# Scaling the attention probabilities on one engine, and copying two levels of linear-attention scores on another

## The chip, the cores and the metric

The kernel runs as one launch on one core of one Trainium2 chip. The metric is the device time of that launch in microseconds (us). Engine names are those of the profile: PE is TensorE (matrix products), DVE is VectorE, ACT is ScalarE, POOL is GpSimd, SP issues DMAs.

## The reference, cut to what matters

The reference is a two-layer decoder trunk on 512 tokens of 1024 features. In each layer three mixers share one input projection and one output projection, and a SwiGLU feed-forward network follows. Two of the mixers matter here.

- **Attention.** Eight heads of 64 columns, in two key groups. Each head has a compressed branch and two full causal branches ("selected" and "window"; with these sizes both see all earlier tokens). For a full branch the output is `gate * softmax(q k^T + causal mask) v`.
- **Gated linear attention (GLA).** Four heads of 32 key and 64 value columns. Inside a block of tokens the score of query i against key j is `sum_d q[i,d] k[j,d] exp(b[i,d] - b[j,d])` for j <= i, with b the running sum of the log-decays; the score matrix then multiplies v.

```
s = jnp.einsum('bqghd,bkgd->bghqk', qb, kwb)
p = masked_softmax(s, wmask[None, None, None])
o_win = jnp.einsum('bghqk,bkgd->bqghd', p.astype(vwb.dtype), vwb)
...
return gb[..., 0:1] * o_cmp + gb[..., 1:2] * o_slc + gb[..., 2:3] * o_win
...
decay = jnp.exp(jnp.where(causal[None, None, :, :, None], diff, -jnp.inf))
attn = jnp.einsum('bhik,bhjk,bhijk->bhij', qc, kc, decay)
o_intra = jnp.einsum('bhij,bhjv->bhiv', attn, vc)
```

## The kernel before, in words

All of the work lies in one function, `trunk_kernel`; `mixer(l, ...)` holds a layer's mixers, `out_proj` the output projection and `ffn` the feed-forward network. Weights come in as float32 tiles, and each is split into a high and a low part, the high one by ACT (L270) and the low one by DVE (L273), so that three products on PE (L285 to L287) give one accurate product. Instruction order is not written by hand: the framework takes program order as priority, moves the weight splits and the evacuations of projections ahead by a fixed offset, and fills each engine's queue by a list schedule. Each engine then works through its queue in order. So matmuls of a projection (L285 to L287) stand between the matmuls of GLA and of attention, as filler.

**GLA.** Each layer has four tiles of 128 tokens (loop over t at L681). DVE forms, for each of seven "levels" (64, 32, 16, 8, 4, 2, 1), a scaled query `xq` (L704) and, for four levels at a time, the scaled keys (L705). For each level one product `xk[level] x xq[level]` (L713) puts 128 keys x (4 heads x 64 queries) of scores into a PSUM bank with tag "t" (two banks in turn). DVE then copies the scores into the matrix `at` under a uint8 mask (L716, `copy_predicated`). The diagonal goes into `at` ahead of that, also on DVE (L708). `at` has two buffers, used in turn; each was set to zero once. Then `at` multiplies the values on PE (L723). At level 64 the masked region is one rectangle: keys 0 to 63 against queries 64 to 127. At level 32 it is two: keys 0 to 31 against queries 32 to 63, and keys 64 to 95 against queries 96 to 127. From level 16 on it is four or more.

ACT's part in a tile: three exponentials (L688), four copies that build the block-diagonal query `qbd` (L691), and the copies L725 and L730.

**Attention.** For each of 8 heads and 2 branches, four query tiles i = 0 to 3 of 128 x 128(i+1) keys: scores on PE (L913, L931 to L933), row maximum on DVE (L917, L935), exponential with row sum on ACT (L921, L937) into a probability tile `P`. DVE then forms the factor `rr`, gate over row sum (L942, L943), and the four tiles are scaled by their column of `rr`:

```
for i in SORD:                       # SORD = (0, 1, 2, 3)
    if i in ISP:                     # ISP = (3,)
        nc.gpsimd.tensor_tensor(ps_[i], ps_[i], rr[:, i : i + 1].to_broadcast(...), op=ALU.mult)   # L946
    else:
        nc.vector.tensor_scalar(ps_[i], ps_[i], rr[:, i : i + 1], None, op0=ALU.mult)              # L948
```

PE transposes the scaled tiles (L954), ACT and DVE split them (L255, L256), PE multiplies with the values (L967, L968). The transposes of key block 0 come first, and they read all four tiles.

Of the kernel before, what the change touches and what calls it, by code (L numbers as in the profile page):

```python
# [16 lines left out]
ALU = mybir.AluOpType  # L17
AX = mybir.AxisListType

P = 128  # L20
# [11 lines left out]
GH = 4  # L32
# [19 lines left out]
NBOTH = 2  # L52
ISP = (3,)
PBK = {"g": 2, "s": 3, "t": 2, "o": 1}
# [7 lines left out]
def shape_constants():  # L62
    """Tables that depend on shapes alone: identity, masks, rotary angles, decay selectors."""
    half = HD // 2
# [15 lines left out]
    i = np.arange(P)  # L80
    tsel = np.zeros((P, 9, P), np.float32)
    lmask = np.zeros((P, 7, 64), np.float32)
    for l, s in enumerate(LEVELS):
        for t in range(P):
            b = t // (2 * s) * (2 * s)
            m = b + s
# [36 lines left out]
def trunk_kernel(ctx: ExitStack, tc: tile.TileContext, a, out):  # L123
# [21 lines left out]

# [1 line left out]
    ident = cp.tile([P, P], F32, name="ident")  # L147
# [77 lines left out]

# [1 line left out]

    def rsqrt(dst, v, n):
        """dst = 1/sqrt(v), v > 0, on [P, n] float32."""
        half_v = small(max(n, NT), "nv", 2)[:, 0:n]  # L230
        nc.vector.tensor_scalar(half_v, v, -0.5, None, op0=ALU.mult)
        ib = small(max(n, NT), "ni", 2, I32)[:, 0:n]
        nc.vector.tensor_scalar(ib, v.bitcast(I32), 1, None, op0=ALU.logical_shift_right)
        nc.vector.tensor_scalar(ib, ib, -1, 0x5F3759DF, op0=ALU.mult, op1=ALU.add)
        y = ib.bitcast(F32)
        t = small(max(n, NT), "nt", 2)[:, 0:n]
        for it in range(3):
            if n == 1:
                nc.vector.scalar_tensor_tensor(t, y, half_v, y, op0=ALU.mult, op1=ALU.mult)
            else:  # L240
                nc.vector.tensor_tensor(t, y, y, op=ALU.mult)
                nc.vector.tensor_tensor(t, t, half_v, op=ALU.mult)
            d = dst if it == 2 else y
            nc.vector.scalar_tensor_tensor(d, t, 1.5, y, op0=ALU.add, op1=ALU.mult)
# [31 lines left out]
    def w_rows(mat, r0, nk, c0, w, pri=WPRI, raw=None, hl=None):  # L276
        """rows r0.. as nk K-tiles of w columns."""
        def loads(raw):
            nc.sync.dma_start(raw[:, 0 : nk * w].rearrange("p (k c) -> p k c", k=nk),
                              mat[r0 : r0 + nk * P, c0 : c0 + w].rearrange("(k p) c -> p k c", p=P))  # L280
        hl = w_unit(nk * w, loads, pri, raw, hl)
        return hl[:, :, 0 : nk * w].rearrange("p s (k c) -> p s k c", k=nk)
# [6 lines left out]
    class Norm:  # L289
        """Sum of squares over features, gathered tile by tile; then 1/rms in both layouts."""  # L290

# [30 lines left out]

# [1 line left out]
    class TokNorm(Norm):  # L324
        """The first norm: sums of squares from x as it comes, token-major."""

# [53 lines left out]
    def residual_out(m, ps, gcols, kts, nrm):  # L380
        """xT[m] += ps, and the next norm's operands from it."""
        nc.vector.tensor_tensor(xT[:, m, :], xT[:, m, :], ps, op=ALU.add)  # L382
        if nrm is not None:
            nrm.add(xT[:, m, :])
            if kts is not None:
                split_scaled(kts[m // 2], m % 2, xT[:, m, :], gcols[:, m : m + 1])

    def o_transposed(src, kt):
        """token-major [P, t, 256] -> kt, feature-major hi/lo."""
        for kk in range(2):  # L390
            ps = psum("t")
            for t in range(NT):
                nc.tensor.transpose(ps[:, t * P : (t + 1) * P], src[:, t, kk * P : (kk + 1) * P], ident)
            split_psum(kt[:, kk, 0, :], kt[:, kk, 1, :], ps)

# [1 line left out]
    def mixer(l, norm, xkt, eu=None):  # L397
# [14 lines left out]
        def proj_tok(units, width, evac, tags="gggg", before=None):  # L412
            """units: list of (view [P, 2, nk, w], first K-tile)."""
            ks = [(u, k0, kk) for u, k0, nk in units for kk in range(nk)]
# [11 lines left out]
        def proj_feat(c0, evac):  # L426
            """two neighbouring 128-column tiles, feature-major."""
            us = [w_rows(w_in, k0 * P, 4, c0, 256) for k0 in (0, 4)]
# [16 lines left out]
        with tc.tile_pool(name=f"mx{l}", bufs=1, reuse_waits="tile") as mp:  # L445
# [13 lines left out]
            with tc.tile_pool(name=f"ma{l}", bufs=1, reuse_waits="tile") as ap:  # L459
                # spatial gating  # L460
                uv = ap.tile([P, NT, SEQ], F32, name=nm("uv"))
# [23 lines left out]
                rb = norm.broadcast()  # L485
                # compressed-branch projections, feature-major
                kvT = [ap.tile([P, SEQ], F32, name=nm("kvT")) for _ in range(2)]
# [30 lines left out]

                # compressed keys and values
                hts = []  # L520
# [71 lines left out]
            with tc.tile_pool(name=f"mg{l}", bufs=1, reuse_waits="tile") as gp:  # L592
# [31 lines left out]

                # decay logits and their log-sigmoid
                zps = psum("s")
# [54 lines left out]
                for t in range(NT):  # L681
# [7 lines left out]
                    for h in range(GH):  # L689
                        r = slice(32 * h, 32 * h + 32)  # L690
                        nc.scalar.copy(qbd[r, h, :], qkT[0][r, tk])  # L691
                    # query side of a level first: the key side then takes its factors' place
                    xqs = []
# [16 lines left out]
                    for lv, s in enumerate(LEVELS):  # L710
                        nb = 64 // s
                        ps = psum("t")[:, 0:256]
                        nc.tensor.matmul(ps, xk[:, lv, :], xqs[lv].rearrange("p h i -> p (h i)"), start=True, stop=True)  # L713
                        av = at.rearrange("p h (b u s) -> p h b u s", u=2, s=s)[:, :, :, 1, :]
                        mv = lmask[:, lv, :].rearrange("p (b s) -> p b s", s=s).unsqueeze(1).to_broadcast([P, GH, nb, s])
                        nc.vector.copy_predicated(av, mv, ps.rearrange("p (h b s) -> p h b s", h=GH, s=s))  # L716
# [34 lines left out]

            # selected and window branches: keys and values
            def ev_b(t, ps):
# [25 lines left out]

# [1 line left out]
            with tc.tile_pool(name=f"mt{l}", bufs=1, reuse_waits="tile") as tp_:  # L781
# [108 lines left out]
                for hp in range(H // 2):  # L890
# [4 lines left out]
                    for hh in range(2):  # L895
# [5 lines left out]
                        for br in range(2):  # L901
# [42 lines left out]
                            for i in SORD:  # L944
                                if i in ISP:
                                    nc.gpsimd.tensor_tensor(ps_[i], ps_[i], rr[:, i : i + 1].to_broadcast([P, P * (i + 1)]), op=ALU.mult)  # L946
                                else:
                                    nc.vector.tensor_scalar(ps_[i], ps_[i], rr[:, i : i + 1], None, op0=ALU.mult)  # L948
                            for js in JG:
# [35 lines left out]
    def out_proj(l, okt, k0, kts, nrm, tags=None):  # L985
        tags = tags or ATAGS
        """xT += rows k0 .. k0 + 3 of the output projection."""
        site("o%d" % k0)
# [18 lines left out]
    def down_tok(l, xt, f0, acts):  # L1007
        """Token-major: xt += one part of the down projection."""
        for h in range(2):
# [12 lines left out]
    def finish(l, fp, xt, f0, acts):  # L1022
        """Token-major: the last part of the down projection, and the final norm."""
        nk = len(acts)
# [117 lines left out]
```

## Time and profile before

| what | value |
|---|---|
| median of 3 runs | 1379.78 us (1379.19 to 1382.06) |
| span of the profiled execution | 1392.3 us |
| PE busy | 1349.9 us, 97% of the span |
| DVE busy | 865.5 us, 62% |
| ACT busy | 533.4 us, 38% |
| POOL busy | 192.9 us, 14% |

The profile is of one execution, and its own time is its span of 1392.3 us; the runs give no separate time for that execution. It is 12.5 us (0.9%) over the median of the three timed runs. Layer 0 has its GLA tiles at about 125 to 167 us and its attention at about 205 to 310 us; layer 1 has them at about 811 to 853 us and 891 to 996 us. The feed-forward networks lie at about 340 to 720 us and from 1031 us on. A busy PE is not a PE at its peak: matmuls are pipelined and their ends are modelled.

### The profile page before, as it was taken

What the parts mean: (1) busy time and instruction counts of PE and PEld (TensorE: products, weight loads), DVE (VectorE), ACT (ScalarE), POOL (GpSimd) and SP (SyncE); (2) the same over time, 40 slices, a digit from 0 to 9 for tenths busy, and PEclk for the clock granted to TensorE, in tenths of its full rate; (3) what the DMA queues carried; (4) which work ended last, traced back from release to release, by engine and by line L of the source; (5) the groups of instructions that cost most, each with busy time, mean ns of one, the idle gap of its engine ahead of it and who ended that gap; (6) DMA issues with size and microseconds to landing.
All of it is one profiled execution on the core that took longest, in us unless ns stands there. A gap on an engine that the chain in (4) does not pass through costs nothing.

```text
span 1392.3 us, 17128 instructions
## 1 busy us (share of the span) xinstructions
PE 1349.9 (97%) x6499; PEld 1098.5 (79%) x6499; DVE 865.5 (62%) x1479; ACT 533.4 (38%) x1020; POOL 192.9 (14%) x166
## 2 busy tenths in 40 slices
PE   7999999999999999999999999999999999999997
PEld 6888776777887888788788777767778888888886
DVE  5546889986554455345654478899765535543455
ACT  6234336664332223123441432567553213222232
POOL 2111021113110011001211111111131100110112
PEclk9889999999999999999997999999999999999999
DMA  8422031002333333332362312200133224323321
GB/s 293 111 80 61 16 107 31 16 16 76 91 105 92 91 106 92 91 93 86 100 186 76 91 33 61 77 16 17 36 89 103 91 76 121 92 90 102 96 90 61
DMA packets 160069, 116.84 MB, mean 84 GB/s; under 512 B 7786, under 2 KB 146804, under 8 KB 159988
## 3 DMA queue, kind: packets, MB, share of 16 engines
q1 hardware_dynamic: 155536, 111.53, 26.9%
q10 hardware_dynamic: 4452, 4.23, 1.0%
q8 instruction: 51, 0.84, 0.2%
q14 instruction: 30, 0.25, 0.1%
HBM read 113.65 MB, written 2.10 MB: 83 GB/s over the span
## 4 chain that ended last, share of the span: by engine, by line
PE 80%; DVE 12%; ACT 4%; issue 3%; DMA 1%; POOL 0%; ACTq 0%; SPq 0%; DVEq 0%
PE psg L285 10%; PE psg L286 10%; PE psg L287 10%; PE pss L285 7%; PE pss L286 7%; PE pss L287 7%; PE pst L286 4%; PE pst L285 4%; PE pst L287 4%; PE pso L543 3%; DVE hl L273 2%; PE pst L954 2%; PE pst L713 2%; ACT hl L270 1%; PE pso L967 1%
## 5 line engine op out<-in xcount | busy, mean ns | idle before, releaser
L270 ACT CAST hl<-raw 128x1024 fp32r<-128x1024 f32 (+2 forms) x186 | 192.8, 1036 | 407.3 <-issue 146.4
L273 DVE TENSOR_TENSOR hl<-raw,hl 128x1024 fp32r<-128x1024 f32 (+2 forms) x186 | 269.0, 1447 | 112.6 <-ACT hl L270 111.5
L285 PE MATMUL psg<-kt,hl 128*128 128x512 f32 x520 | 208.1, 401 | 3.4 <-DVE xT L382 3.4
L286 PE MATMUL psg<-kt,hl 128*128 128x512 f32 x520 | 207.8, 400 | 0.0
L287 PE MATMUL psg<-kt,hl 128*128 128x512 f32 x520 | 207.0, 398 | 0.0
L286 PE MATMUL pss<-kt,hl 128*128 128x512 f32 x376 | 146.7, 390 | 0.0
L285 PE MATMUL pss<-kt,hl 128*128 128x512 f32 x376 | 146.4, 389 | 0.0
L287 PE MATMUL pss<-kt,hl 128*128 128x512 f32 x376 | 146.3, 389 | 0.0
L1087 POOL TENSOR_TENSOR ft<-ft,ft 128x512 f32<-128x512 f32 x44 | 56.7, 1288 | 600.9 <-DVE ft L1086 588.2
L285 PEld LDWEIGHTS psg<-kt,hl 128*128 128x128 f32 x520 | 99.0, 191 | 22.9 <-DVE xT L382 4.2
L286 PEld LDWEIGHTS psg<-kt,hl 128*128 128x128 f32 x520 | 99.4, 191 | 19.4 <-issue 0.5
L287 PEld LDWEIGHTS psg<-kt,hl 128*128 128x128 f32 x520 | 99.3, 191 | 19.1
L1086 DVE SCALAR_TENSOR_TENSOR ft<-pss,rb 128x512 f32<-128x512 f32 x44 | 30.4, 691 | 128.0 <-PE pss L287 128.0
L285 PE MATMUL psg<-hl,kt 128*128 128x512 f32 (+2 forms) x288 | 107.2, 374 | 1.3 <-ACT hl L270 0.8
L286 PE MATMUL psg<-hl,kt 128*128 128x512 f32 (+2 forms) x288 | 105.1, 366 | 0.0
L287 PE MATMUL psg<-hl,kt 128*128 128x512 f32 (+2 forms) x288 | 105.1, 366 | 0.0
L285 PEld LDWEIGHTS pss<-kt,hl 128*128 128x128 f32 x376 | 70.6, 188 | 14.6
L287 PEld LDWEIGHTS pss<-kt,hl 128*128 128x128 f32 x376 | 70.6, 188 | 14.4
L286 PEld LDWEIGHTS pss<-kt,hl 128*128 128x128 f32 x376 | 70.6, 188 | 14.4
L255 ACT CAST act<-ft 128x512 fp32r<-128x512 f32 x44 | 27.4, 622 | 115.2 <-DVE ft L1088 115.2
L285 PE MATMUL pst<-act,hl 128*128 128x512 f32 x176 | 69.5, 396 | 0.8 <-ACT act L255 0.8
L286 PE MATMUL pst<-act,hl 128*128 128x512 f32 x176 | 69.9, 397 | 0.3
(330 smaller groups left out, 2502.0 us busy)
## 6 DMA issues: line engine op xcount, KB each, us to landing
raw<-in_w_gate_dram SPq DMA_DIRECT2D x44, 512.0 KB, 3.9
raw<-in_w_up_dram SPq DMA_DIRECT2D x44, 512.0 KB, 3.9
raw<-in_w_down_dram SPq DMA_DIRECT2D x38, 512.0 KB, 3.8
raw<-in_w_in_dram SPq DMA_DIRECT2D x32, 512.0 KB, 3.7
raw<-in_w_out_dram SPq DMA_DIRECT2D x16, 512.0 KB, 3.9
w<-in_cmp_w_k_dram SPq DMA_DIRECT2D x16, 256.0 KB, 4.5
w<-in_cmp_w_v_dram SPq DMA_DIRECT2D x16, 256.0 KB, 2.7
raw<-in_w_down_dram SPq DMA_DIRECT2D x8, 384.0 KB, 3.3
```

The source lines that it names most:

```text
L255: nc.scalar.copy(hi, src)
L270: nc.scalar.copy(hl[:, 0, 0:n], raw[:, 0:n])
L273: e_.tensor_tensor(hl[:, 1, 0:n], raw[:, 0:n], hl[:, 0, 0:n].bitcast(F32), op=ALU.subtract)
L285: nc.tensor.matmul(ps, lh, rh, start=start, stop=False)
L286: nc.tensor.matmul(ps, lh, rl, start=False, stop=False)
L287: nc.tensor.matmul(ps, ll, rh, start=False, stop=stop)
L543: nc.tensor.matmul(ps[:, hh * 62 : (hh + 1) * 62], wu[:, kk, hh * P : (hh + 1) * P], bf[:, s, :], start=s == 0 and hh == 0, stop=s == 15 a ...
L713: nc.tensor.matmul(ps, xk[:, lv, :], xqs[lv].rearrange("p h i -> p (h i)"), start=True, stop=True)
L954: nc.tensor.transpose(T[:, c : c + P], ps_[i][:, j * P : (j + 1) * P], ident)
L967: nc.tensor.matmul(O[:, j * P : SEQ], lhs, pt[:, 0, c : c + n], start=first, stop=False)
L1086: nc.vector.scalar_tensor_tensor(ux, pss[1], 0.5, rb, op0=ALU.mult, op1=ALU.mult)
L1087: nc.gpsimd.tensor_tensor(ux, ux, gx, op=ALU.mult)
```

## The change

Two edits. First, all four probability tiles of a branch are scaled by DVE with the same `tensor_scalar`; the POOL instruction is gone (32 in all: 8 heads x 2 branches x 2 layers). Second, at levels 64 and 32 the scores are copied from PSUM into `at` by ACT, one plain copy for each rectangle (one of 64 partitions x 256 elements, two of 32 partitions x 128 elements), in place of a masked copy of 128 x 256 by DVE (16 masked copies become 24 plain ones: 2 layers x 4 tiles). The rest of the difference is comments and docstrings, left out here; they only shift the line numbers.

```diff
-ISP = (3,)
...
                         av = at.rearrange("p h (b u s) -> p h b u s", u=2, s=s)[:, :, :, 1, :]
+                        if lv < 2:
+                            for b_ in range(nb):
+                                kr_ = slice(2 * s * b_, 2 * s * b_ + s)
+                                nc.scalar.copy(av[kr_, :, b_, :], ps[kr_].rearrange("p (h b s) -> p h b s", h=GH, s=s)[:, :, b_, :])
+                            continue
                         mv = lmask[:, lv, :].rearrange("p (b s) -> p b s", s=s).unsqueeze(1).to_broadcast([P, GH, nb, s])
                         nc.vector.copy_predicated(av, mv, ps.rearrange("p (h b s) -> p h b s", h=GH, s=s))
...
                             for i in SORD:
-                                if i in ISP:
-                                    nc.gpsimd.tensor_tensor(ps_[i], ps_[i], rr[:, i : i + 1].to_broadcast([P, P * (i + 1)]), op=ALU.mult)
-                                else:
-                                    nc.vector.tensor_scalar(ps_[i], ps_[i], rr[:, i : i + 1], None, op0=ALU.mult)
+                                nc.vector.tensor_scalar(ps_[i], ps_[i], rr[:, i : i + 1], None, op0=ALU.mult)
```

## Rows read from the trace of the kernel before

**Rows 1.** The page: span, busy slices, and the chain that ended last.
```profile
span 1392.3 us, 17128 instructions
...
PE   7999999999999999999999999999999999999997
...
PE 80%; DVE 12%; ACT 4%; issue 3%; DMA 1%; POOL 0%; ACTq 0%; SPq 0%; DVEq 0%
```
**Rows 2.** Windows by stage: length, then each engine's busy us, PE clock, DMA.
```profile
125.00:167.00 42.00, 41.10 (x189) 30.51 (x188) 36.59 (x93) 11.40 (x34) 1.59 (x2) 1.00 0.06 19
811.00:853.00 42.00, 41.09 (x189) 30.53 (x189) 36.72 (x93) 11.25 (x33) 1.59 (x2) 1.00 0.06 21
...
205.00:310.00 105.00, 100.52 (x584) 76.13 (x583) 98.10 (x223) 71.67 (x202) 17.71 (x16) 1.00 0.08 25
340.00:720.00 380.00, 378.86 (x1662) 309.71 (x1661) 190.75 (x218) 110.20 (x140) 40.49 (x30) 1.00 0.35 101
891.00:996.00 105.00, 100.61 (x586) 76.35 (x586) 98.44 (x223) 72.08 (x202) 17.72 (x16) 1.00 0.08 25
```
**Rows 3.** The chain by line, in 125 to 167 us and in 205 to 310 us.
```profile
by line: PE pst L713 26.0%; DVE at L716 11.4%; PE psg L285 10.6%; PE psg L286 9.5%; PE psg L287 8.8%; PE pso L723 7.3%; DVE xq L704 4.1%; PE pso L721 3.6%; DVE E L705 3.0%; DVE hl L273 2.9%; PE pst L732 2.6%; issue 1.6%; DVE at L708 1.6%; P
...
by line: PE pst L954 11.8%; PE pso L967 8.3%; DVE P L948 7.5%; PE pso L968 7.0%; DVE PT L256 5.4%; PE psg L285 5.1%; PE psg L287 4.9%; PE psg L286 4.7%; ACT PT L255 4.3%; PE pss L931 4.0%; PE pss L932 3.9%; issue 3.6%; DVE qst L831 3.2%; PE
```
**Rows 4.** The masked copies on DVE: their group, then two lines of DVE's timeline.
```profile
L716 DVE COPY_PREDICATED at<-m,pst 128x256 f32<-128x256 uint8 x56 | 28.8, 514 | 1.7 <-PE pst L713 1.0
...
129.28 0.44 DVE L716 COPY_PREDICATED at<-m,pst 128x256 f32<-128x256 uint8 x1
129.61 0.41 DVE L704 TENSOR_TENSOR xq<-qbd,E 128x256 f32<-128x256 f32 x1
```
**Rows 5.** Copies from PSUM on ACT, by line and shape: busy us, mean ns, idle before.
```profile
L725 ACT COPY osb<-pso 128x256 f32<-128x256 f32 x8 | 3.0, 372 | 9.2 <-PE pso L723 9.2
...
L730 ACT COPY tmp<-pst 128x128 f32<-128x128 f32 x6 | 1.6, 266 | 12.6 <-PE pst L728 12.6
```
**Rows 6.** Waits of DVE for ACT in 205 to 310 us: total us, times, longest.
```profile
DVE PT L256 <- ACT PT L255: 3.6, 9, 1.0
```
**Rows 7.** The scalings: DVE's and POOL's groups, then L948 with min/median/max ns.
```profile
L948 DVE TENSOR_SCALAR P<-P,rr 128x128 f32<-128x128 f32 x32 | 15.1, 472 | 0.4
L948 DVE TENSOR_SCALAR P<-P,rr 128x256 f32<-128x256 f32 x32 | 14.5, 454 | 0.0
L948 DVE TENSOR_SCALAR P<-P,rr 128x384 f32<-128x384 f32 x32 | 13.1, 409 | 0.0
...
L946 POOL TENSOR_TENSOR P<-P,rr 128x512 f32<-128x512 f32 x32 | 35.4, 1107 | 174.5 <-DVE rr L943 134.5 <-ACT P L937 22.5 <-ACT hl L270 10.1
...
L948 DVE TENSOR_SCALAR P<-P,rr x96: 274/405/1131, 210.4 to 994.2; 128x128 f32<-128x128 f32 x32, 128x256 f32<-128x256 f32 x32, 128x384 f32<-128x384 f32 x32
```
**Rows 8.** Timeline of DVE: three scalings (128, 256, 384 columns), POOL idle beside them.
```profile
275.34 0.87 DVE L948 TENSOR_SCALAR P<-P,rr 128x128 f32<-128x128 f32 x3
276.13 1.14 DVE L935 TENSOR_REDUCE nmx<-pss 128x1 f32<-128x384 f32 x2
```
**Rows 9.** Timelines of DVE and of POOL: the same three scalings, POOL busy beside them.
```profile
304.07 1.66 DVE L948 TENSOR_SCALAR P<-P,rr 128x128 f32<-128x128 f32 x3
305.65 0.16 DVE L942 RECIPROCAL rr<-den 128x4 f32<-128x4 f32 x1
...
304.20 1.05 POOL L946 TENSOR_TENSOR P<-P,rr 128x512 f32<-128x512 f32 x1 [8.22 <-DVE rr L943]
```
**Rows 10.** DVE's group of the same operation at 512 columns.
```profile
L1056 DVE TENSOR_SCALAR xt<-yg,rstd 128x512 f32<-128x512 f32 x4 | 1.9, 487 | 0.4
```
**Rows 11.** Waits of PE for the scalings in 205 to 310 us.
```profile
PEld pst L954 <- DVE P L948: 2.0, 4, 0.8
...
PE pst L954 <- DVE P L948: 1.3, 3, 0.6
```
**Rows 12.** Timeline of ACT in a GLA tile: four copies of L691 in a row.
```profile
131.03 1.26 ACT L691 COPY qbd<-gqk 32x128 f32<-32x128 f32 x4 [4.78 <-DVE xq L704]
```

## The prediction, made before the changed kernel was run

> **What bounds the kernel now.** I read the page first [rows 1]: PE is at least nine tenths busy in nearly every slice, and the chain that ended last is 80% PE and 12% DVE, with POOL at 0%. Next come the windows by stage [rows 2]. The reader is to see that the change falls into stages of their own. In a feed-forward stretch PE is busy 378.9 of 380 us and DVE only half of it, so nothing that DVE saves there could be felt, and the change touches nothing there. In each GLA stage (42 us) PE is busy 41.1 us and DVE 36.6; in each attention stage (105 us) PE 100.5 and DVE 98.1. Both engines are close to full, and which of them ends last must be read from the chain within the stage [rows 3]. In GLA the PE lines that the row names sum to 68.4% of the 42 us, the masked copies L716 hold 11.4%, and the other DVE lines named 11.6%. In attention PE leads again, and the scalings L948 hold 7.5% of 105 us.
>
> From this I take a rule for pricing DVE's work: the share of a line's busy time that lies on the chain. L716 is busy 28.8 us in all [rows 4], 14.4 in a layer, and 11.4% of 42 us is 4.8 us on the chain: 33%. L948 is busy 15.1 + 14.5 + 13.1 = 42.7 us [rows 7], 21.4 in a layer, and 7.5% of 105 us is 7.9 us: 37%. The rest of either has PE's in-order stream of filler products beside it.
>
> The sum is made in differences against the profiled execution, whose own time is its span of 1392.3 us [rows 1]; that is 12.5 us above the median of the runs, 1379.78 us. I apply the difference to the median. A measurement of this kernel can tell about 0.2% from no change: 2.8 us.
>
> **GLA: 16 masked copies leave DVE.** Of the seven copies of a tile, those of levels 64 and 32 go. A masked copy runs 0.44 us, and the next DVE instruction starts 0.33 us after it [rows 4]: DVE is freed 16 x 0.33 = 5.3 us. On the chain 33% of that counts: -1.8 us. The ends: nothing (PE's filler alone sets the pace) and the whole -5.3.
>
> ACT gains 24 copies. The trace has no such copy of 64 or 32 partitions; the nearest are copies from PSUM of 256 columns, 372 ns, and of 128 columns, 266 ns [rows 5]. A tile costs ACT 0.37 + 2 x 0.27 = 0.91 us, 3.6 in a layer. ACT is busy 11.4 of 42 us there [rows 2], so I cost this time at nothing: idle ACT hides it. Where that cover is gone, it is 7.2 us over both layers.
>
> The edit adds a hand-off. The diagonal (L708, DVE) must be in `at` before ACT writes, and DVE's level-16 copy writes the same columns and so waits for ACT's last copy. Queued behind it on DVE are the next scaled queries and level copies, and PE's L713 and L723 wait for those. A hand-off of this kind is priced by another pair, where DVE waits for ACT to read the same bank first: 3.6 us in 9 waits, 0.4 each [rows 6]. One per tile makes 8 x 0.4 = 3.2 us. It can also gain: DVE puts a scaled query between two copies [rows 4], while ACT may free the PSUM bank at once, one slot of 0.33 us a tile, 8 x 0.33 = 2.6 us. I take 0, since DVE has scaled queries of later levels to do in the meantime, and keep +3.2 and -2.6 for the range.
>
> **Attention: 32 scalings move from POOL to DVE.** Alone, the three scalings of a branch take DVE 0.79 us from the first start to the next instruction [rows 8]. With POOL beside them they take 1.58 us (304.07 to 305.65), and they do not get through until POOL's 1.05 us is over [rows 9]. Over all branches: the shortest scaling is 274 ns and is of 128 columns; the 384-column group, scaled last, is close to undisturbed at 409; halfway, 341, is the 256-column one. The groups' means are 472 and 454, so contention costs (472 - 274) + (454 - 341) = 311 ns a branch, 10.0 us over 32 [rows 7]. That goes.
>
> The Trainium skill ("SBUF — State Buffer", section "Who interferes with whom") says why: a two-port DVE operation and a GpSimd operation exclude each other, and the later one fully blocks. The trace agrees; its longest scaling is 1131 ns.
>
> What comes is a fourth scaling. The same operation at 512 columns takes 487 ns [rows 10]; instructions in a row overlap by some 0.08 us (three end after 0.87, the next starts at 0.79 [rows 8]), so 0.41 us of DVE, 32 x 0.41 = 13.1 us. Net on DVE +3.1 us, and 37% of it counts: +1.1 us. The ends: all of +3.1, if DVE paces the stage, and 37% of -10.0, that is -3.7, if the added scalings all fall into DVE's idle time (105 - 98.1 = 6.9 us a layer [rows 2], room for 6.6). The transposes of key block 0 read all four tiles, so the last of them is late next: where POOL collided, all four are ready after about 0.79 + 0.41 = 1.2 us instead of 1.6; where it did not, 0.4 us later than three were. POOL's 35.4 us vanish off the chain: worth nothing by themselves. No DMA moves.
>
> **Order.** The list schedule may deal all queues anew, since instructions change engines. No row shows what that costs. What it could return at most is PE's idle time in the four stages, 2 x (0.9 + 4.5) = 10.8 us [rows 2]; I take 0 and let it widen both ends.
>
> **Sum.** -1.8 + 0 + 1.1 = -0.7 us: 1379.1 us, no measurable change.
>
> **The rivals.**
>
> *DVE paces GLA (faster).* The freed time counts whole, -5.3 us, and attention stays even: 1374.5 us. For it: the copies on the chain, and DVE at 36.6 of 42 us. Against: PE at 41.1 of 42. With attention at its best end (PE waits for L948 3.3 us in layer 0 [rows 11], and those shrink) it is -5.3 - 3.7: 1370.8 us.
>
> *ACT's queue delays the early levels (slower).* Place: the copies of levels 64 and 32 stand in ACT's in-order queue. The four `qbd` copies of the next tile, 1.26 us, wait themselves for DVE [rows 12]; if they stand ahead, PSUM banks and the level-16 copy wait behind them. Price 8 x 1.26 = 10.1 us; in half of the tiles 5.0, so -0.7 + 5.0 gives 1384.1 us, and in all of them 1389.2. It decides once the block is ahead in over a third of the tiles. Against: ACT is three quarters idle in that stage.
>
> *DVE paces attention, PE paces GLA (slower).* +3.1 and 0: 1382.9 us.
>
> *POOL's help was worth its whole time (slower).* If the long scalings were long for another reason, 10.0 us do not come back, and 37% of 13.1 is +4.8 - 1.8: 1382.8 us; whole, 1391.1. Rows 9 speak against it [rows 9]. The Trainium skill ("Perfetto Trace Analysis", section "Optimizing Scalar/DVE Operations") advises to offload a saturated DVE, even to GpSimd, which is this rival's case; it adds that the shared port may undo that, as the trace shows.
>
> **How the numbers follow.** Chances: forecast 0.42; DVE paces GLA 0.30; ACT's queue 0.15; DVE paces attention 0.08; POOL's help 0.05. The forecast's own range is 1377 to 1382.5 us. The whole range, 1371 to 1388 us, takes in the fast end of the second case and most of the ACT case. Faster by over 0.2%: 0.30. Slower by over 0.2%: 0.15 + 0.08 + 0.05 = 0.28. Within: 0.42.
>
> **What would show it.** Right: no L946; L948 as 128 instructions with means near 274, 341, 409 and 487 ns and none above 600 (busy near 32 x 1.51 = 48 us); L716 as 40; ACT up by 7 us; POOL down by 35.4 us; GLA windows 42 us within 1, attention 105 within 2. Wrong in GLA: windows shorter by over 2 us, or waits of DVE's L716 on the new ACT copies of over 3 us. Wrong in attention: windows longer by over 3 us with PE waiting on L948. Anything beyond 1371 or 1388 us would mean that the reordering, which I cost at nothing, decides.

## The result, and the profile after

The changed kernel takes 1393.47 us (median of 4 runs, 1387.48 to 1395.25) against 1380.42 us for the kernel before (median of 4, 1379.19 to 1382.06): 1.0084 times as long, 95% interval 1.0055 to 1.0112. It is slower by 13.05 us, and 5.5 us beyond the upper end of the range. In all that follows, medians and ratios leave out the executions over 1.5% above a kernel's fastest: six of before's, and one of the GLA copies alone, which took 1481.4 us at a mean clock of 0.843 and is the one profiled of that kernel, so that no row of it is shown. In the changed program the line numbers have moved: the scaling is L950, the masked copy L721, the new ACT copy L718, the transposes L956, the value products L969 and L970, ACT's and DVE's split L254 and L255.

The page of the kernel after (span; busy times, share and instructions; PE's slices; the chain by engine):

```profile
span 1393.5 us, 17072 instructions
...
PE 1343.5 (96%) x6499; PEld 1091.2 (78%) x6499; DVE 865.4 (62%) x1495; ACT 539.4 (39%) x1044; POOL 159.6 (11%) x134
...
PE   7999999999999999999999999989999999999997
...
PE 79%; DVE 11%; ACT 5%; issue 3%; DMA 1%; POOL 0%; ACTq 0%; SPq 0%; DVEq 0%
```

It answers to [rows 1], and the reader is to see how little it shows: PE was 97% busy and is 96%, and the chain is 79% PE for 80%. POOL's 192.9 us fell to 159.6, as 32 instructions of 1.1 us should let them. The page does not say where 13 us came from.

A cut of layer 1 at five marks does. The marks are DVE's first scaled query, ACT's last copy `osb`, DVE's first factor `rr`, the last head's addition (before: L704, L725, L943, L981), and the feed-forward network's first gated product (L1084). So the four rows are GLA, the stretch to attention, attention, and the **tail**, which is the rest of the output projection. Columns as in [rows 2]: the window, its length, busy time (instructions) of PE, its weight loads, DVE, ACT and POOL, PE's granted clock, DMA. The kernel after, windows by stage:

```profile
805.70:844.80 39.10, 37.90 (x177) 28.14 (x176) 32.78 (x84) 13.37 (x43) 2.64 (x2) 1.00 0.06 16
844.80:890.20 45.40, 43.59 (x215) 34.65 (x213) 37.71 (x73) 20.14 (x37) 8.66 (x6) 1.00 0.30 93
890.20:998.30 108.10, 100.60 (x567) 75.78 (x567) 97.70 (x234) 69.34 (x191) 0.00 (x0) 0.98 0.07 20
998.30:1035.50 37.20, 34.90 (x160) 27.80 (x158) 24.85 (x38) 16.92 (x25) 11.54 (x7) 1.00 0.31 94
```

The kernel before, the same four stages:

```profile
811.60:852.70 41.10, 40.19 (x185) 29.78 (x184) 36.12 (x93) 10.54 (x32) 1.59 (x2) 1.00 0.05 15
852.70:896.40 43.70, 41.51 (x208) 33.24 (x206) 37.90 (x73) 19.59 (x36) 8.45 (x6) 1.00 0.30 96
896.40:1001.40 105.00, 100.61 (x582) 76.45 (x582) 95.70 (x217) 69.48 (x191) 17.72 (x16) 1.00 0.07 21
1001.40:1034.40 33.00, 31.31 (x145) 25.01 (x143) 24.14 (x38) 17.14 (x25) 10.72 (x7) 1.00 0.36 108
```

- **GLA** is 2.0 us shorter (41.1 to 39.1), and the stretch after it 1.7 longer. PE has 8 matmuls less in the first (177 for 185) and 7 more in the second.
- **Attention** is 3.1 us longer, 105.0 to 108.1, of which about 1 us is a short stretch at a lower clock (mean 0.98; another trace of the same two edits, shown below, has 1.00 and 107.0). That stretch, 3.4 us at 0.5, is no accident of this trace. It stands 21 to 22 us into attention in four of the six attention stages of the kernels that move the whole scaling to DVE and nothing else in attention (the changed kernel, both edits again, the scaling alone), and in none of the 18 of before and the other kernels below, the GLA copies alone left aside. Up to it PE was busy 19.3 of this stage's first 21.3 us, where before it was busy 19.7 of 21.2.
- **The tail** is 4.2 us longer, 33.0 to 37.2, though the change touches no line that runs there. PE has 160 matmuls in it for 145, and 567 for 582 in attention. Fifteen products (L285 to L287, the output projection's filler) left attention and are done after it, when there is no other work for them to be hidden behind.

The feed-forward networks kept their 309.5 and 311.2 us (first to last gated product; 309.6 and 311.2 after). With layer 1 counted twice, the tail gives about 8.2 us, attention 4.0 (at the full clock), GLA and the stretch behind it -0.6: 11.6 of the 13.05 us. The stretches at the lower clock in attention are most of the rest: by the same marks, layer 0 takes 6.0 us more in the four stages (224.8 to 230.9) and layer 1 7.0, together 13.0.

The scalings themselves came out as forecast. The groups of DVE in the kernel after, by line and shape (busy us, mean ns, idle before):

```profile
L950 DVE TENSOR_SCALAR P<-P,rr 128x512 f32<-128x512 f32 x32 | 15.4, 481 | 0.1
L950 DVE TENSOR_SCALAR P<-P,rr 128x384 f32<-128x384 f32 x32 | 13.3, 415 | 0.0
L950 DVE TENSOR_SCALAR P<-P,rr 128x256 f32<-128x256 f32 x32 | 11.1, 348 | 0.0
L950 DVE TENSOR_SCALAR P<-P,rr 128x128 f32<-128x128 f32 x32 | 9.0, 281 | 0.2
```

The three that stood beside POOL had means of 472, 454 and 409 ns [rows 7]; they have 281, 348 and 415, and the fourth takes 481. The longest of the 128 is 491 ns, where it was 1131.

### The profile page after: what moved, and what is told of

It reads as the page before. It is cut to its first block, busy times and chain, and to the rows that moved or that the text cites. A ratio compares the mean times of both kernels' runs of the same rounds, so it can differ in the third digit from the quotient of the medians.

```text
span 1393.5 us, 17072 instructions
## 1 busy us (share of the span) xinstructions
PE 1343.5 (96%) x6499; PEld 1091.2 (78%) x6499; DVE 865.4 (62%) x1495; ACT 539.4 (39%) x1044; POOL 159.6 (11%) x134
## 4 chain that ended last, share of the span: by engine, by line
PE 79%; DVE 11%; ACT 5%; issue 3%; DMA 1%; POOL 0%; ACTq 0%; SPq 0%; DVEq 0%
PE psg L284 9%; PE psg L285 9%; PE psg L286 9%; PE pss L284 7%; PE pss L285 7%; PE pss L286 7%; PE pst L285 4%; PE pst L284 4%; PE pst L286 4%; DVE hl L272 2%; PE pso L542 2%; PE pst L956 2%; PE pso L969 2%; PE pso L970 1%; PE pst L712 1%
## 5 line engine op out<-in xcount | busy, mean ns | idle before, releaser
L285 PE MATMUL psg<-kt,hl 128*128 128x512 f32 x520 | 205.9, 396 | 0.7 <-DVE kt L250 0.7
L285 PE MATMUL pss<-kt,hl 128*128 128x512 f32 x376 | 146.3, 389 | 0.0
L285 PEld LDWEIGHTS psg<-kt,hl 128*128 128x128 f32 x520 | 98.4, 189 | 20.4 <-DVE kt L250 1.2
L285 PE MATMUL psg<-hl,kt 128*128 128x512 f32 (+2 forms) x288 | 105.2, 365 | 0.4 <-DVE hl L272 0.4
L285 PEld LDWEIGHTS pss<-kt,hl 128*128 128x128 f32 x376 | 70.6, 188 | 14.6
L254 ACT CAST act<-ft 128x512 fp32r<-128x512 f32 x44 | 27.4, 622 | 116.4 <-DVE ft L1090 116.4
L285 PE MATMUL pst<-act,hl 128*128 128x512 f32 x176 | 69.9, 397 | 0.3 <-DVE act L255 0.2
```

The source lines that it names most:

```text
L254: nc.scalar.copy(hi, src)
L285: nc.tensor.matmul(ps, lh, rl, start=False, stop=False)
```

## The experiments

Eleven kernels ran. Three theories were put up. **Theory 1**: the list schedule, dealing DVE's queue anew, takes filler out of attention, and this is paid after it. **Theory 2**: the fourth scaling's time on DVE is the price. **Theory 3**: the loss lies in GLA, in the hand-off from ACT to DVE. Where a text speaks of filler in a layer's attention, it counts the products L285 to L287 in the order of the program: 97 before, 82 after, in the four quarters (two heads each) 25, 23, 25, 24 before and 20, 11, 24, 27 after. Times of before are medians of 24, 30 and 22 runs: 1380.21 us for the first four kernels, 1380.80 for the next four, 1383.93 for the last three. The granted clock differs from run to run and moves these medians by a few us, so runs of equal mean clock are set side by side where that matters. The window rows below are all of layer 1, attention and then the tail; before has 105.0 and 33.0 us.

**The scaling alone.**

```diff
-ISP = (3,)
+ISP = ()
```

> Only the scaling moves to DVE; linear attention as before. Order read from the built program: 82 products of the output projection stand between the first and the last attention instruction of PE in a layer, 97 before. Theory 1 (lost filler: residual adds stand later in DVE's queue, projection banks stay held, 15 products a layer run after attention instead of within it): about 11 to 14 us slower than before, two attention windows longer by 2 to 3 us each and two tails of the output projection longer by 3.5 us each. Theory 2 (the fourth scaling's time on DVE, 13.1 - 10.0 = 3.1 us, and later tiles): 3 to 5 us slower. Theory 3 (the loss is in linear attention, ACT's hand-off): no change within 2 us.

Measured: 1395.05 us, 1.0099 times before (1.0064 to 1.0133). Its attention and tail:

```profile
889.60:997.80 108.20, 100.69 (x567) 75.82 (x567) 97.64 (x233) 69.34 (x191) 0.00 (x0) 0.98 0.07 20
997.80:1035.00 37.20, 34.94 (x159) 27.79 (x157) 24.81 (x38) 16.88 (x25) 11.54 (x7) 1.00 0.30 93
```

These are the changed kernel's rows within 0.1 us. The whole loss is here.

**The GLA copies alone.** Levels 16 and finer keep the masked copy.

```diff
-                        mv = lmask[:, lv, :].rearrange("p (b s) -> p b s", s=s).unsqueeze(1).to_broadcast([P, GH, nb, s])
...
+                        if lv in (0, 1): [nc.scalar.copy(av[2 * s * b_ : 2 * s * b_ + s, :, b_, :], ps[2 * s * b_ : 2 * s * b_ + s].rearrange("p (h b s) -> p h b s", h=GH, s=s)[:, :, b_, :]) for b_ in range(nb)]
```

> Only the ACT copies; scaling as before (POOL takes tile 3). The built order has 56 products of the projection in each linear-attention stage instead of 64, and 8 more right behind it; attention keeps its 97. Theories 1 and 2: within 2 us of before, the stage 2 us shorter in each layer and the stretch behind it longer by about as much (8 x 0.23 = 1.8 us). Theory 3 (ACT's hand-off costs): 5 to 13 us slower.

Measured: 1386.26 us, 1.0025 times before (0.9995 to 1.0055): no change that can be told. Most of its runs had a lower clock than before's; at equal clock the two agree within 2 us (at 0.990 1382.1 and 1382.6 us, before 1380.8 to 1382.8; at 0.996 1374.0, before 1375.7 and 1376.0). With the run before, theory 3 falls.

**Both edits again**, written into the kernel before so that its line numbers stay.

```diff
-ISP = (3,)
+ISP = ()
...
+                        if lv in (0, 1): [nc.scalar.copy(av[2 * s * b_ : 2 * s * b_ + s, :, b_, :], ps[2 * s * b_ : 2 * s * b_ + s].rearrange("p (h b s) -> p h b s", h=GH, s=s)[:, :, b_, :]) for b_ in range(nb)]
```

> The changed kernel once more, with the line numbers of before: both edits. All theories: about 1393 us, 0.8% slower than before; this is the comparison for the next kernel.

Measured: 1394.4 us, 1.0103 (1.006 to 1.0146): the change's loss again. This trace has the full clock in attention, so it is the one to set beside before:

```profile
890.70:997.70 107.00, 99.52 (x568) 74.76 (x568) 97.67 (x234) 69.53 (x191) 0.00 (x0) 1.00 0.07 21
997.70:1034.80 37.10, 34.81 (x159) 27.77 (x157) 24.80 (x37) 16.85 (x25) 11.52 (x7) 1.00 0.31 94
```

Attention is 2.0 us longer and DVE's busy time in it 1.97 us (95.70 to 97.67). PE is busy 1.1 us less with 14 matmuls less. The tail is 4.1 us longer.

Cut into quarters, from the first factor `rr` of every second head, the stage shows where PE lacks filler. The second quarter before, and with both edits:

```profile
926.70:954.00 27.30, 26.57 (x159) 20.30 (x159) 26.34 (x61) 18.76 (x54) 4.16 (x4) 1.00 0.01 1
...
920.50:946.70 26.20, 23.66 (x143) 18.28 (x142) 24.96 (x64) 17.74 (x53) 0.00 (x0) 1.00 0.01 1
```

With 16 matmuls less, PE is idle 2.5 us of this quarter, where it was idle 0.7; DVE is idle 1.2 and 1.0.

**Both edits, and the first half of the output projection evacuated early.** The residual additions (L382) of that half, which empty the filler's PSUM banks, are given a higher priority in the list schedule; filler in attention as the program is ordered: 106.

```diff
-                residual_out(2 * mq + b, ps, g_ffn(l), kts, nrm)
+                with tc.high_priority(offset=400 if k0 == 4 else 0): residual_out(2 * mq + b, ps, g_ffn(l), kts, nrm)
```

> Both edits, and the residual adds of the first half of the output projection are given the priority offset that the weight splits have (400), so that DVE's queue has them earlier. Same instructions and same durations as the changed kernel, another order: the built program has 106 filler products in a layer's attention instead of 82. Theory 1: 24 products a layer move back under attention, 2 x 24 x 0.23 = 11 us, so 1380 to 1384 us. Theory 2: within 3 us of the changed kernel, 1390 to 1396 us, since the scalings on DVE are the same.

Measured: 1387.34 us, 1.0052 (1.0022 to 1.0083). No instruction differs from the kernel above, only their order, and half of the loss is gone:

```profile
884.80:993.90 109.10, 102.77 (x591) 78.94 (x591) 97.95 (x233) 70.13 (x191) 0.00 (x0) 1.00 0.07 20
993.90:1026.60 32.70, 30.16 (x135) 23.24 (x133) 24.56 (x37) 17.09 (x25) 11.08 (x7) 1.00 0.37 107
```

The tail is back at 32.7 us; attention has 591 matmuls for 568 and is 2.1 us longer. So the order is a cause, and it is not the only one.

**No fourth scaling at all.** The scaling of the widest tile is left out, and with it POOL's part in attention; the rest of each queue stands in the order of the kernel before.

```diff
-ISP = (3,)
+ISP = ()
...
-                            for i in SORD:
+                            for i in SORD[0:3]:
```

> The widest tile (512 columns) is not scaled at all, by POOL or by DVE: that part of the computation is left out. Everything else stands in the order of the kernel before (25, 23, 25 and 24 filler products in the four quarters of a layer's attention). It shows what POOL's scalings cost DVE by themselves, with nothing re-dealt. Theory 1 (the order decides): within 3 us of before, 1377 to 1383, since nothing is re-dealt. Theory 2 (DVE's scaling time decides): 32 groups x 0.31 us of contention = 10 us of DVE work are gone, of which 37% to all are on the path: 1370 to 1376.

Measured: 1376.57 us, 0.9965 (0.9945 to 0.9985), 4.2 us under before; at an equal clock of 0.992 it is 5.6 (1374.8, three runs, for 1380.3, four).

```profile
879.60:981.80 102.20, 99.28 (x582) 76.64 (x582) 91.32 (x217) 69.47 (x191) 0.00 (x0) 1.00 0.07 22
981.80:1014.80 33.00, 31.32 (x145) 25.00 (x143) 24.14 (x38) 17.12 (x25) 10.65 (x7) 1.00 0.36 107
```

DVE's busy time falls from 95.70 to 91.32 us, 8.8 us over both layers: this is what POOL's scalings cost DVE, and the prediction's 10.0 us was near. Attention is 2.8 us a layer shorter, the tail the same to 0.1 us. Theory 1 alone forecast no change, so theory 2 has a part: DVE's time in attention counts, and not at 37% but at 2.8 of 4.4, 64%. It is not a wait for POOL that went: nothing waited for POOL's scaling in the trace of before.

**The fourth scaling cut to 128 columns.** The other 384 of the widest tile are left unscaled. Filler as ordered: 97 (37, 28, 4, 28).

```diff
-ISP = (3,)
+ISP = ()
...
-                                    nc.vector.tensor_scalar(ps_[i], ps_[i], rr[:, i : i + 1], None, op0=ALU.mult)
+                                    nc.vector.tensor_scalar(ps_[i][:, 0 : P if i == 3 else P * (i + 1)], ps_[i][:, 0 : P if i == 3 else P * (i + 1)], rr[:, i : i + 1], None, op0=ALU.mult)
```

> All scalings on DVE, but of the widest tile only the first 128 of 512 columns: the rest is left unscaled, which is the part left out. DVE has the same number of instructions as with the fourth scaling whole, 32 x (0.48 - 0.28) = 6.4 us less of work, and the build's order keeps 97 filler products in a layer's attention as before (with the fourth scaling whole it is 82), dealt 37, 28, 4, 28. Theory 1: at or near before, 1378 to 1384, some 12 to 15 us under the kernel with only the scaling moved (1395.05). Theory 2: only the 6.4 us less work counts, 1388 to 1393.

Measured: 1384.72 us, 1.0017 (0.9989 to 1.0045), 3.9 us over before: no change that can be told.

```profile
886.20:991.80 105.60, 101.23 (x582) 76.40 (x582) 93.98 (x234) 69.22 (x191) 0.00 (x0) 1.00 0.07 21
991.80:1024.70 32.90, 31.24 (x144) 24.95 (x142) 24.09 (x38) 17.09 (x25) 10.63 (x7) 1.00 0.36 106
```

It has the DVE instructions of the scaling alone, 6.4 us less work in them, and 582 and 144 matmuls in place of 567 and 159. It is 10.9 us nearer to before by the medians (3.9 for 14.8 over its own before), and 11.2 by the rows at the full clock (a layer's attention and tail take 138.5 us, and 144.1 with both edits). Not even the whole 6.4 us would explain that: theory 2 alone falls as well.

**The scaling alone, with the first half evacuated somewhat early.** Filler as ordered: 99 (20, 11, 24, 44).

```diff
-ISP = (3,)
+ISP = ()
...
-                residual_out(2 * mq + b, ps, g_ffn(l), kts, nrm)
+                with tc.high_priority(offset=200 if k0 == 4 else 0): residual_out(2 * mq + b, ps, g_ffn(l), kts, nrm)
```

> Only the scaling moved to DVE, whole, and the out-projection's residual additions of its first half built with a priority 200 higher: the same instructions as the kernel with only the scaling moved, but 99 filler products in a layer's attention instead of 82, the additional ones in the last quarter (20, 11, 24, 44). Theory 1, if only the sum of fillers counts: 1378 to 1383. Theory 1, if their place counts (quarter two still has 11 for 23): 1384 to 1390. Theory 2: unchanged, 1393 to 1397.

Measured: 1387.92 us, 1.0047 (1.0013 to 1.008).

```profile
881.20:989.70 108.50, 102.58 (x584) 77.19 (x584) 97.88 (x234) 69.48 (x191) 0.00 (x0) 1.00 0.07 20
989.70:1023.20 33.50, 31.40 (x143) 24.57 (x141) 24.60 (x38) 17.13 (x25) 10.56 (x7) 1.00 0.36 104
```

This is the clean pair for the order: the instructions of the scaling alone, all four scalings whole on DVE. Attention takes 17 matmuls more (584 for 567) in 0.3 us more (1.5 against the full-clock 107.0), and the tail falls from 37.2 to 33.5. So a filler product costs about 0.09 us inside attention (1.5 us for 17), and outside it 0.23 (3.7 us for 16). What is left over before, 7.1 us, is attention's 3.5 us a layer. DVE has 2.2 us more there than before, but the added time stands in the last quarter, where PE is the full engine. The second and the last quarter of attention:

```profile
910.90:937.10 26.20, 23.64 (x143) 18.27 (x142) 24.96 (x63) 17.73 (x53) 0.00 (x0) 1.00 0.00 1
...
962.10:989.70 27.60, 27.59 (x152) 21.03 (x152) 21.67 (x52) 14.97 (x38) 0.00 (x0) 1.00 0.07 20
```

and the last quarter before:

```profile
978.00:1001.40 23.40, 22.73 (x128) 17.55 (x127) 18.12 (x42) 13.02 (x34) 4.20 (x4) 1.00 0.00 1
```

The filler came back in the last quarter alone. There PE has no idle time left while DVE is idle 5.9 us, and this quarter is 4.2 us longer than before; in the second quarter PE is idle 2.6 us, as it is with both edits (2.5). So the place of the filler counts beside its sum, as the second form of theory 1 had it (1384 to 1390 us).

**The fourth scaling on ACT.** Filler as ordered: 101 (31, 12, 24, 34).

```diff
-                                    nc.gpsimd.tensor_tensor(ps_[i], ps_[i], rr[:, i : i + 1].to_broadcast([P, P * (i + 1)]), op=ALU.mult)
+                                    nc.scalar.activation(ps_[i], ps_[i], AF.Copy, scale=rr[:, i : i + 1])
```

> The widest tile is scaled by ACT (an activation with a per-partition scale) instead of POOL or DVE; linear attention is as before. The build's order has 101 filler products in a layer's attention (31, 12, 24, 34). Theory 1: at or under before, 1374 to 1382. Theory 2: DVE loses 10 us of contention and gains no work: 1370 to 1376. If ACT's queue becomes the bound instead (its 32 scalings of about 0.5 to 0.9 us delay exponentials and evacuations): 1385 to 1400.

Measured: 1387.45 us, 1.0022 (0.9995 to 1.005): no change that can be told. The median is 6.6 us over before's because most of its runs had a lower clock; at 0.990 three of it average 1381.8 us and five of before 1381.7.

```profile
881.50:986.50 105.00, 100.92 (x586) 78.08 (x586) 91.33 (x217) 79.31 (x207) 0.00 (x0) 1.00 0.07 21
986.50:1019.60 33.10, 31.16 (x141) 24.24 (x139) 24.65 (x38) 17.02 (x25) 10.83 (x7) 1.00 0.36 107
```

DVE is at 91.33 us as without the fourth scaling, yet attention is as long as before. Theory 2's forecast of 1370 to 1376 fails here: where ACT's queue holds another 10 us, DVE idles 13.7 us instead of 9.3.

**Two scalings on ACT.** Tiles of 384 and 512 columns. Filler as ordered: 103 (35, 22, 22, 24).

```diff
-ISP = (3,)
+ISP = (2, 3)
...
-                                    nc.gpsimd.tensor_tensor(ps_[i], ps_[i], rr[:, i : i + 1].to_broadcast([P, P * (i + 1)]), op=ALU.mult)
+                                    nc.scalar.activation(ps_[i], ps_[i], AF.Copy, scale=rr[:, i : i + 1])
```

> Tiles of 384 and 512 columns are scaled by ACT, those of 128 and 256 by DVE, none by POOL; linear attention as before. Order as built: 103 filler products in a layer's attention, dealt evenly (35, 22, 22, 24). Theory 1 and 2 together (DVE's time and filler both count): DVE has 32 x 0.42 = 13 us less than the kernel without the fourth scaling, at least as many fillers, so 1370 to 1378. If ACT's queue bounds (32 x 0.73 + 32 x about 0.57 = 42 us more on ACT, whose share of attention was 69 of 105 us): 1380 to 1392.

Measured: 1372.93 us, 0.9908 (0.9877 to 0.994). It beats both kernels.

```profile
874.00:976.80 102.80, 101.08 (x588) 76.82 (x588) 86.86 (x201) 86.17 (x223) 0.00 (x0) 1.00 0.07 22
976.80:1009.50 32.70, 30.80 (x138) 23.78 (x136) 24.58 (x38) 17.10 (x25) 11.10 (x7) 1.00 0.36 108
```

PE is busy 101.1 of 102.8 us, DVE 86.9: of the whole-stage rows shown, this is where PE comes nearest to setting the pace of attention. Its two groups on ACT (busy us, mean ns, idle before):

```profile
L946 ACT ACTIVATE P<-P,rr 128x512 f32<-128x512 f32 x32 | 23.2, 725 | 0.0
...
L946 ACT ACTIVATE P<-P,rr 128x384 f32<-128x384 f32 x32 | 19.9, 623 | 0.0
```

The layer's two rows are 2.5 us shorter than before's, 5.0 us over both layers, of the 11.0 us by which the medians differ. The rest is the granted clock, which was higher in this kernel's six runs than in most of before's: where both had 0.997, three runs of it average 1369.8 us and two of before 1373.9, a gain of 4.1 us. So the version's own gain is 4 to 5 us.

**Two scalings on ACT, and the GLA copies.**

```diff
-ISP = (3,)
+ISP = (2, 3)
...
-                                    nc.gpsimd.tensor_tensor(ps_[i], ps_[i], rr[:, i : i + 1].to_broadcast([P, P * (i + 1)]), op=ALU.mult)
+                                    nc.scalar.activation(ps_[i], ps_[i], AF.Copy, scale=rr[:, i : i + 1])
...
+                        if lv in (0, 1): [nc.scalar.copy(av[2 * s * b_ : 2 * s * b_ + s, :, b_, :], ps[2 * s * b_ : 2 * s * b_ + s].rearrange("p (h b s) -> p h b s", h=GH, s=s)[:, :, b_, :]) for b_ in range(nb)]
```

> As the kernel with two tiles scaled by ACT, with linear attention's 64 and 32 key levels copied by ACT as well. Linear attention's gain of 2.1 us a layer was given back by 8 deferred filler products: within 1.5 us of the kernel with two tiles on ACT alone. If the copies' gain is kept where attention is less short of DVE: 2 to 4 us under it.

Measured: 1375.5 us, 0.9942 (0.9908 to 0.9976). The copies add nothing that can be told: what GLA gains (39.6 us for 41.6 in the kernel without them), the stretch behind it gives back (45.0 for 43.3).

**The fourth scaling on DVE, the third on ACT.** Filler as ordered: 102 (26, 21, 18, 37).

```diff
-ISP = (3,)
+ISP = (2,)
...
-                                    nc.gpsimd.tensor_tensor(ps_[i], ps_[i], rr[:, i : i + 1].to_broadcast([P, P * (i + 1)]), op=ALU.mult)
+                                    nc.scalar.activation(ps_[i], ps_[i], AF.Copy, scale=rr[:, i : i + 1])
```

> The 512-column tile is scaled whole by DVE, as in the change, but the 384-column tile by ACT; POOL scales none. DVE has 32 x (0.48 - 0.41) = 2 us more than the kernel without the fourth scaling, and the build deals 102 filler products evenly (26, 21, 18, 37). Theory 2 by DVE's sum of work alone: 1378 to 1381. Theory 1 by filler alone: 1376 to 1382, far from 1395 too. A result above 1388 would say that the place of the 512-column scaling on DVE, last ahead of the transposes, is what costs.

Measured: 1379.11 us, 0.9958 (0.9932 to 0.9985).

```profile
883.10:987.30 104.20, 100.54 (x587) 77.90 (x587) 92.42 (x218) 77.16 (x207) 0.00 (x0) 1.00 0.07 21
987.30:1019.80 32.50, 30.84 (x139) 23.88 (x137) 24.59 (x38) 17.15 (x25) 10.90 (x7) 1.00 0.37 109
```

The 512-column scaling that the change adds to DVE is in this kernel whole, and it is faster than before. So the place of that scaling, last ahead of the transposes, is not by itself what costs. Against the scaling alone with early evacuation, DVE has 5.5 us a layer less and attention is 4.3 us shorter, at 587 and 584 matmuls: again most of what DVE is freed of, though the filler is also dealt more evenly here (26, 21, 18, 37 for 20, 11, 24, 44).

## Why the prediction was wrong

**"Order": the step that failed.** The prediction wrote "No row shows what that costs [...] I take 0 and let it widen both ends". The tail, which the change does not touch, is 4.1 us longer in each layer, 8.2 in both. The runs show the order as the cause: with the same instructions and another priority for the additions that empty the filler's banks, the tail goes from 37.2 to 33.5 us, and the kernel is 7.1 us over before and not 14.8. The bound of 10.8 us that the prediction gave for a gain (PE's idle time) was no bound for a loss. In the order of DVE's queue the fourth scaling stands ahead of those additions and of the splits (L273) of the next weights; both have lower priority, so with DVE full the list schedule puts them later, and with them the filler that needs their banks and weights. The traces show the additions late: of the six in a layer's attention, the four quarters hold 2, 1, 3 and 0 before, and 1, 0, 2 and 3 after. The rest of that chain of causes is argued from the order of the queue: PE's waits in attention name no wait of the filler for a bank or for weights, since the schedule had moved it already. What the runs show is that raising the additions undoes the longer tail. The prediction's last sentence, that a result beyond 1388 us "would mean that the reordering, which I cost at nothing, decides", came true: raising the additions alone takes back about half of the loss (7.7 of 14.8 us).

**Attention, +1.1: mis-sized, about +4.0.** The net work was right: +3.1 us over both layers, measured 2 x (97.67 - 95.70) = 3.9. What failed is the 37% by which it was to count: leaving the fourth scaling out gives 64%. The +4.0 itself is no clean price of DVE's work, since the filler was dealt anew in the same stage. The windows of [rows 2] also lie about 5 us ahead of the stage; by the marks, DVE's idle time in it was 9.3 us and not 6.9. That idle time is nearly the same in the kernels that scale on DVE alone, or on DVE and POOL: 105.0 - 95.7 = 9.3 us before, 9.3 with both edits, 10.9 without the fourth scaling, 11.6 at 128 columns, 10.6 and 11.2 with early evacuation. So the stage's length goes with DVE's whole queue, to within these 2.3 us and not more closely: at 128 columns DVE has 1.7 us less work than before, and attention is 0.6 us longer. The chain's share of one line says only how often that line ended last. The chain by line in attention, layer 1, after:

```profile
by line: PE pst L956 13.6%; PE pso L969 10.8%; PE pso L970 8.4%; ACT PT L254 7.5%; PE pss L936 5.9%; PE psg L284 5.3%; PE psg L286 5.0%; PE pss L937 4.9%; PE psg L285 4.9%; PE pss L918 4.0%; issue 3.5%; DVE PT L255 2.9%; DVE P L950 2.7%; AC
```

and before:

```profile
by line: PE pst L954 10.5%; PE pso L967 8.1%; DVE P L948 7.5%; PE pso L968 7.1%; DVE PT L256 6.4%; PE psg L285 4.6%; ACT PT L255 4.4%; PE psg L286 4.3%; PE psg L287 4.2%; issue 3.5%; PE pss L931 3.4%; PE pss L932 3.3%; DVE nmx L935 3.2%; PE
```

The scalings' share of it even fell, from 7.5% to 2.7%, in a stage that became longer by what DVE was given. What rose is PE's own dependent work and ACT's split (4.4% to 7.5%). The waits of PE's weight loads (total us, times, longest) show the same, after:

```profile
PEld pso L969 <- ACT PT L254: 10.5, 26, 0.9
...
PEld pst L956 <- DVE P L950: 1.6, 8, 0.3
```

and before:

```profile
PEld pso L967 <- ACT PT L255: 6.6, 20, 0.7
...
PEld pst L954 <- DVE P L948: 2.0, 4, 0.8
```

PE stands waiting for the split, 10.5 us in 26 waits for 6.6 in 20. That it does so for want of filler between a transpose and the value products is argued; the sum of the filler is not enough for it, since with the additions early and 584 matmuls the waits are still 9.7 us in 27. The late scaling that the prediction feared grew no wait: 1.6 us for 2.0. So the price came out in waits for other work than the scalings. Which of DVE's instructions stands behind each of them is not shown.

**DVE paces attention: the rival that was half right.** It had 0.08 and +3.1 us for attention, against 4.0 measured. It left the order out as well, and so gave 1382.9 us.

**POOL's contention, 10.0 us: right.** Without POOL beside them DVE is freed of 8.8 us, and the two attention stages are 5.6 us shorter. The rival that these 10 us would not come back is refuted.

**GLA, -1.8: near in the sum, by luck.** DVE is freed of 3.3 us a layer there (36.12 to 32.78), 6.7 in both, near the 5.3 forecast, and the stage is shorter by 2.0 us a layer, 60% and not 33%. But 8 filler products moved behind the stage with it (185 matmuls to 177), and the stretch there grew by 1.7 us; net -0.6 us in the kernel. The larger gain and the filler moved behind the stage, both unforeseen, nearly cancel. The copies on ACT (busy us, mean ns, idle before):

```profile
L718 ACT COPY at<-pst 32x128 f32<-32x128 f32 x16 | 4.1, 254 | 2.1 <-PE pst L712 1.9
...
L718 ACT COPY at<-pst 64x256 f32<-64x256 f32 x8 | 2.9, 366 | 9.4 <-PE pst L712 9.4
```

366 and 254 ns, where 372 and 266 were taken from the nearest rows [rows 5]. The waits about them, GLA of layer 1 (total us, times, longest):

```profile
ACT at L718 <- PE pst L712: 5.7, 6, 2.6
...
PEld pst L712 <- ACT at L718: 1.3, 5, 0.4
```

ACT waits for PE, 5.7 us, more than PE for ACT, 1.3 us in 5 waits; and the rival of ACT's queue, 1384.1 us, did not come about.

**What was to be seen.** Right: no POOL scaling, 128 scalings on DVE with the four means, 48.8 us against 48, 40 masked copies, ACT up by 6.0 us (7 forecast), POOL down by 33.3 (35.4 forecast). At the edge or beyond: "attention 105 within 2" (107.0 to 108.1), with no longer wait of PE on the scalings, and "GLA windows 42 us within 1" (2.0 us shorter by the marks).

**What stays open.** No run had the whole fourth scaling on DVE and exactly the order of before, so the split of 8 and 4 us rests on stage lengths, and part of the 4 may be the order's too: at the 64% above, DVE's 3.9 us would cost 2.5, an estimate. How the dealing over the quarters matters was not tried by itself; the quarters' rows show only that it does.

## What to carry to other kernels

Where instructions are ordered by a static list schedule, an instruction that moves to a nearly full engine is paid for by whatever stands behind it with lower priority: count the filler of each stage in the new order before taking "reordering" at nothing. Count where it stands, too: filler that came back in a quarter where PE had no idle time left did not make up for the quarter that lacked it. Do not price work on such an engine by the share of one line on the chain that ended last; its whole queue time came nearer here. And if an engine is to be freed, give the work to one with room: two scalings moved to ACT took DVE from 95.7 to 86.9 us and left PE busy 101.1 of 102.8 us, where the whole set on DVE cost 13 us. The Trainium skill ("Perfetto Trace Analysis", section "Optimizing Scalar/DVE Operations") says the like: a saturated DVE may hand work to Scalar, while GPSIMD shares a port with it. The traces agree on both (the longest scaling fell from 1131 to 491 ns once POOL was gone), with one limit: the 512-column scaling alone on ACT, 725 ns for DVE's 481, gained nothing that could be told.

## What the runs showed of the hardware that was not expected

The granted clock alone spreads the times of one kernel by more than the change did. The kernel before took 1373.4 us at a mean clock of 0.997 and 1391.7 at 0.982. The difference comes in stretches at the lower of the clock's two levels (1.2 GHz of 2.4), such as this one in the profile of before, far ahead of the change (columns as above):

```profile
39.00:59.40 20.40, 19.14 (x109) 16.56 (x107) 16.83 (x37) 6.41 (x16) 4.15 (x5) 1.00 0.41 117
59.40:76.50 17.10, 17.10 (x78) 16.70 (x78) 4.59 (x10) 0.92 (x3) 0.00 (x0) 0.50 0.32 92
```

and the same stretch in the kernel with two scalings on ACT:

```profile
39.00:59.40 20.40, 19.18 (x110) 16.68 (x109) 16.46 (x36) 6.05 (x16) 4.16 (x5) 1.00 0.38 113
59.40:76.50 17.10, 16.31 (x137) 15.54 (x136) 5.13 (x11) 1.13 (x4) 0.00 (x0) 1.00 0.30 93
```

In 17.1 us PE got through 78 matmuls at 0.50 and 137 at 1.00; ahead of it PE was 19.1 and 19.2 of 20.4 us busy in the two. The profiled execution of before had more such time (mean clock 0.980, its span 12.5 us above the median) than the one after (0.987). That is why the spans of the two profiles, 1392.3 and 1393.5 us, hide the loss, and why stages at clock 1.00 are compared here.
